# Another order of all engines, one load per block at the head, fewer tiny steps and quarter columns at the end of a hybrid decoder layer

## The chip, the cores and the metric

The kernel runs on one core of a Trainium2 chip. The core has a matrix engine (TensorE, PE in the profile), a vector engine (VectorE, DVE), a scalar engine (ScalarE, ACT), GpSimd (POOL) and SyncE (SP), which here only issues transfers; GpSimd issues some as well. The metric is the device time of one execution in microseconds (us), the median over several runs. Everything is fp32 at the interface.

## What is computed

One decoder layer for 512 tokens of width 1024. One combined projection of x feeds two causal mixers; they are merged by gates, projected, added to x and normalised; a gated MLP with a short convolution follows, with a second residual and norm.

```python
h = x @ w_in                                   # q, 6 key/value sets, gates, GDN q/k/v, beta, decay, gate, merge gates
nsa = nsa_attention(...)                       # 8 heads of 64: compressed, selected and window branches, per-head gates
gdn = gated_deltanet(...)                      # 4 heads of 128, chunks of 64, conv 4, triangular solve, gated RMSNorm
mix = sigmoid(g1) * (nsa @ w_nsa_out) + sigmoid(g2) * (gdn @ w_gdn_out)
x = layer_norm(alpha * x + mix @ w_o, ln1_g, ln1_b)
u = causal_dwconv(x @ w_up, conv_w)            # 2 x 2816 columns, width 3
ffn = (act(u[..., :2816]) * u[..., 2816:]) @ w_down
out = layer_norm(alpha * x + ffn, ln2_g, ln2_b)
```

## The kernel before, in words

**Products.** An fp32 operand is split into a rounded high part and the remainder (`split_block`, L447 to L454; `split_w`, L460 to L471; `split`, L1176 and L1177): ScalarE rounds, VectorE subtracts. Each product is then three matmuls, high × high (L481), low × high (L483) and high × low (L484, all in `product`). A full matmul has a moving operand of 512 columns.

**Head.** `load_all` (L433 to L437) loads the transposed x in eight blocks of 128 rows (`xr`), the first two in halves, and beside them the 288 columns of those weights that need the output token by token (`wB`), one block or two at a time. `token_major` multiplies each block with them for four tiles of 128 tokens into the PSUM tiles `pb` (L536 to L538, 12 matmuls a block). Small tables are loaded among these: `tiny` (convolution taps, decays and the like), `pos`, `ident` (for transposes), `fcw`, `cst`.

**Projections and mixers.** `gemm_t` makes one unit of the combined projection: it loads 512 KB of weights (`raw`), splits them and runs 24 matmuls a tile into a PSUM buffer `gps`, of which there are two. Between these units lie the small steps of DeltaNet (`gdn_k`, `gdn_q`, `gdn_v`, `gdn_mid`, the triangular solve with `xs` and `z` at L769 to L772, `gdn_out` with 128-wide matmuls at L837 to L861, `gdn_gate` with `so`, `y` and `yT`) and of the attention (scores L1039 and L1040, softmax `sc` L1043 to L1056, transposes L1072, products with v L1086 and L1092). Most of their matmuls are 64 to 256 wide.

**Merge.** For each of eight channel pairs, two `gps` units give the gate by a tanh (L1118, on ScalarE, into `mt`), the two mixers' outputs are projected into the PSUM tiles `pm0` and `pm1`, VectorE multiplies them in (L1196, one for each) and adds the two (L1198). The tile `mt` is then free for another unit's tanh, and that tanh frees a `gps` buffer.

**o-products and FFN.** The output projection runs as fast-product halves of seven sub-products into `pu` and `pw` (L1285), added into the residual by VectorE at L1290, with its bn_stats at L1292. The up-projection goes the same way; the down-projection is `three` at L1449 into `px` and `pz`, with weight sums formed by transfers on GpSimd's queue. At the end `take` (L1482) adds a 128 × 512 tile of `px` into the residual, `count` takes its bn_stats (L1491), `norm` aggregates (L1241), gets the reciprocal root (L1243, then a power on GpSimd, L522), scales (L1249, L1250) and stores (L1496).

**What sets the order.** The program is written stage by stage, but the order on each engine is not that of the code: QUEUES holds for each engine a list of instruction numbers, and `queues` chains them, so that the scheduler keeps that order. These chains carry no semaphore: an instruction waits on the chip only for its data and buffers.

## Time and profile before

| | us |
|---|---|
| runs | 822.28, 822.27, 820.61 |
| median | 822.27 |
| span of the profiled execution | 820.8 |
| TensorE busy in it | 802.4 (98%) |
| VectorE busy | 600.2 (73%) |
| ScalarE busy | 409.1 (50%) |
| GpSimd busy | 179.7 (22%) |

The profile gives the span of its execution, from the first instruction to the end of the last store; a time that includes what lies around it is known only for the three runs. A row of a table of stretches gives the stretch, its length, then for each engine the busy time and the number of instructions, then TensorE's granted clock, the share of time that the DMA engines were busy, and the rate in GB/s. A timeline row gives start, duration, engine, line, operation, output <- input and shape; several equal instructions in a row are drawn as one, with "x4" at the end; in brackets stands how long the engine had stood idle, and what released it. The queue of transfers is SPq.

### The profile page before, as it was taken

How to read it: one execution, taken by the hardware profiler on the slowest of the kernel's cores; microseconds unless marked ns; L12 is line 12 of the kernel's file. 1: busy time of each engine (PE TensorE's matmuls, PEld its weight loads, DVE VectorE, ACT ScalarE, POOL GpSimd, SP SyncE). 2: the span in 40 equal slices, each digit the busy share in tenths (PEclk: the TensorE clock that was granted, in tenths of full speed). 3: DMA queues.
4: the chain of work that ended last, by engine and by line, in shares of the span. 5: the costliest groups of instructions: out<-in, count | busy, mean ns of one | idle time of the engine just before them, and what ended most of it. 6: DMA issues, size and time to landing. Idle time of an engine off the chain costs nothing.

```text
span 820.8 us, 11781 instructions
## 1 busy us (share of the span) xinstructions
PE 802.4 (98%) x4138; PEld 670.2 (82%) x4138; DVE 600.2 (73%) x1339; ACT 409.1 (50%) x912; POOL 179.7 (22%) x176
## 2 busy tenths in 40 slices
PE   8999999999999999999999999999999999999996
PEld 8788888787888888888787898888888888878784
DVE  5667689979768965556578956666685667777888
ACT  4453587774577764323254234344354444565641
POOL 0244835042365111241200101111111210200000
PEclk9999999999999999999999999999999999999999
DMA  8327280013624942343357387285336492465674
GB/s 282 106 78 267 80 267 30 26 53 97 161 86 103 194 90 77 108 134 123 103 209 226 129 168 243 93 185 146 98 117 210 111 235 91 143 202 178 210 220 149
DMA packets 43978, 119.57 MB, mean 146 GB/s; under 512 B 3472, under 2 KB 4624, under 8 KB 43664
## 3 DMA queue, kind: packets, MB, share of 16 engines
q1 hardware_dynamic: 32144, 87.37, 33.3%
q0 software_dynamic: 11776, 31.46, 16.6%
q8 instruction: 32, 0.52, 0.3%
q14 instruction: 26, 0.21, 0.1%
HBM read 116.72 MB, written 33.55 MB: 183 GB/s over the span
## 4 chain that ended last, share of the span: by engine, by line
PE 79%; DVE 9%; DMA 7%; ACT 2%; issue 2%; SPq 0%; POOL 0%; DVEq 0%; ACTq 0%; POOLq 0%
PE pu L481 9%; PE pu L483 9%; PE pu L484 9%; PE gps L481 9%; PE gps L483 8%; PE gps L484 8%; DMA raw<-wsum 3%; PE pout L1086 2%; PE aps L1072 2%; DMA raw<-in_down 2%; DVE wl L1385 2%; PE pz L1449 2%; PE pm L483 2%; PE pm L481 2%; PE pm L484 2%
## 5 line engine op out<-in xcount | busy, mean ns | idle before, releaser
L471 DVE TENSOR_TENSOR wl<-raw,wh 128x512 fp32r<-128x512 f32 x146 | 103.9, 717 | 73.2 <-ACT wh L467 40.9
L467 ACT ACTIVATE wh<-raw 128x512 fp32r<-128x512 f32 x126 | 79.0, 629 | 138.6 <-PE pu L483 91.4
L484 PE MATMUL pu<-mh,wl 128*128 128x512 f32 (+1 forms) x384 | 129.9, 372 | 0.2 <-DVE wl L471 0.2
L481 PE MATMUL pu<-mh,wh 128*128 128x512 f32 (+1 forms) x384 | 129.8, 372 | 0.0
L483 PE MATMUL pu<-ml,wh 128*128 128x512 f32 (+1 forms) x384 | 129.6, 372 | 0.0
L481 PE MATMUL gps<-xh,wh 128*128 128x512 f32 x320 | 123.5, 399 | 2.4 <-ACT mt L1118 1.5
L483 PE MATMUL gps<-xl,wh 128*128 128x512 f32 x320 | 123.2, 397 | 0.0
L484 PE MATMUL gps<-xh,wl 128*128 128x512 f32 x320 | 122.8, 397 | 0.0
L484 PEld LDWEIGHTS pu<-mh,wl 128*128 128x128 f32 x384 | 71.3, 188 | 13.4 <-DVE wl L471 0.6
L481 PEld LDWEIGHTS pu<-mh,wh 128*128 128x128 f32 x384 | 71.0, 188 | 12.6
L483 PEld LDWEIGHTS pu<-ml,wh 128*128 128x128 f32 x384 | 71.0, 188 | 12.6
L1407 DVE SCALAR_TENSOR_TENSOR fa<-pu,fcw,fa 128x511 f32<-128x511 f32 (+1 forms) x88 | 64.9, 745 | 18.9 <-ACT fa L1404 18.3
L1413 POOL TENSOR_TENSOR fth<-fth,fa 128x512 f32<-128x512 f32 x22 | 31.3, 1428 | 197.3 <-DVE fth L1412 182.8
L481 PEld LDWEIGHTS gps<-xh,wh 128*128 128x128 f32 x320 | 60.0, 188 | 13.5 <-issue 2.9
L484 PEld LDWEIGHTS gps<-xh,wl 128*128 128x128 f32 x320 | 60.0, 188 | 11.0 <-POOL wl L471 0.2
L483 PEld LDWEIGHTS gps<-xl,wh 128*128 128x128 f32 x320 | 60.1, 188 | 10.6
L1384 ACT ACTIVATE wh<-raw 128x512 fp32r<-128x512 f32 x67 | 40.0, 625 | 37.2 <-DMA raw<-wsum 11.4
L1385 DVE TENSOR_TENSOR wl<-raw,wh 128x512 fp32r<-128x512 f32 x67 | 44.5, 691 | 15.8 <-ACT wh L1384 15.3
L1404 ACT ACTIVATE fa<-pu,fcw 128x512 f32<-128x512 f32 x44 | 29.5, 681 | 30.7 <-PE pu L484 29.2
L471 POOL TENSOR_TENSOR wl<-raw,wh 128x512 fp32r<-128x512 f32 x30 | 40.0, 1337 | 13.5 <-ACT wh L467 7.1
L522 POOL TENSOR_TENSOR rs<-rs,minus_half 128x1 f32<-128x1 f32 x8 | 7.6, 949 | 155.9 <-DVE rs L1243 103.2
L1045 ACT ACTIVATE sc<-sc,mn 128x384 f32<-128x384 f32 (+2 forms) x64 | 35.6, 558 | 5.7 <-DVE mn L1043 5.2
(365 smaller groups left out, 1702.1 us busy)
## 6 DMA issues: line engine op xcount, KB each, us to landing
raw<-in_up SPq DMA_DIRECT2D x44, 512.0 KB, 3.7
raw<-in_wT SPq DMA_DIRECT2D x40, 512.0 KB, 3.5
wsum<-in_down POOLq DMA_DIRECT2D x6, 2816.0 KB, 21.7
raw<-wsum SPq DMA_DIRECT2D x20, 512.0 KB, 4.3
raw<-in_down SPq DMA_DIRECT2D x15, 512.0 KB, 3.9
osum<-in_wo POOLq DMA_DIRECT2D x6, 1024.0 KB, 9.4
wsum<-wsum POOLq DMA_DIRECT2D x2, 2816.0 KB, 14.2
raw<-in_wm SPq DMA_DIRECT2D x8, 512.0 KB, 3.5
```

Of the source, the lines that this page charges most:

```text
L467: A.activation(wh, r, AF.Copy)
L471: eng.tensor_tensor(wl, r, wh.bitcast(F32), op=OP.subtract)
L481: i = PE.matmul(ps, wh[k], mh_(k), start=(k == 0), stop=False)
L483: PE.matmul(ps, wh[k], ml_(k), start=False, stop=False)
L484: PE.matmul(ps, wl[k], mh_(k), start=False, stop=(k == n - 1))
L1045: A.activation(s[:, i, :n], s[:, i, :n], AF.Exp, scale=-1.0, bias=mn[:, 0, i:i + 1], accum_out=mn[:, 1, i:i + 1])
L1072: PE.transpose(pt[:, i, k, :], s[:, i, k * 128:(k + 1) * 128], ident)
L1384: A.activation(hi, raw[:, i], AF.Copy)
L1385: V.tensor_tensor(lo, raw[:, i], hi.bitcast(F32), op=OP.subtract)
L1404: A.activation(acc, ps, AF.Copy, scale=w[:, 2:3])
L1407: V.scalar_tensor_tensor(acc[:, n:], ps[:, :S - n], w[:, i:i + 1], acc[:, n:], op0=OP.mult, op1=OP.add)
L1413: G.tensor_tensor(th, th, g[1], op=OP.mult)
```

## The change

It has four parts.

1. *Head loads.* On the host x and the 288 columns are put side by side as `xw`, 800 columns for each block of 128 rows. One transfer of 400 KB brings a block; only the first block comes in three pieces (256, 288 and 256 columns) and is split in halves. The tables move behind the blocks; `pos` becomes 32 columns of `tiny`; the norm's rows are broadcast on the host.
2. *Fewer tiny steps.* `hbeta` is gone. A polynomial of 16 VectorE steps in `decays` takes 9. `norms` becomes `squares`: q's sum of squares isn't turned into a reciprocal root any more, but goes as a term into the one of the output gate, whose chain of five small VectorE steps is now one. `gk` starts from a reciprocal.
3. *Quarter columns at the end.* For the last token tile, the last two pairs of w_down rows are multiplied for 256 columns at a time into `pz0` and `pz1`, and added and counted quarter by quarter; the part before them is taken in as a half as before.
4. *Order.* All five tables of QUEUES are new, and a string TURNS gives one order over all engines, chained in the same way, without semaphores.

The core of the diff, the tables left out but for two lines:

```diff
-        xr = [es.tile([128, S], F32, name=f"xr{k}") for k in range(KD)]
-        raw = [es.tile([128, 2, 288], F32, name=f"wB{k}") for k in range(KD // 2)]
+        xw = [es.tile([128, S + 288], F32, name=f"xw{k}") for k in range(KD)]
         for k in range(KD):
-            n = 2 if k < 2 else 1
-            for i in range(n):
-                ts = slice(i * S // n, (i + 1) * S // n)
-                nc.sync.dma_start(out=xr[k][:, ts], in_=d["xT"][:, k, ts])
-                if i == 0 and k < 2:
-                    nc.sync.dma_start(out=raw[0][:, k], in_=d["wB"][:, k, :])
-                elif i == 0 and k % 2 == 0:
-                    nc.sync.dma_start(out=raw[k // 2], in_=d["wB"][:, k:k + 2, :])
-        return xr, [r[:, i] for r in raw for i in range(2)]
+            for cs in (slice(0, 256), slice(512, 800), slice(256, 512)) if k == 0 else (slice(0, 800),):
+                nc.sync.dma_start(out=xw[k][:, cs], in_=d["xw"][k, :, cs])
+        return [t[:, :S] for t in xw], [t[:, S:] for t in xw]
...
-        V.tensor_scalar(acc, z2, 2.0 / 17, 2.0 / 15, op0=OP.mult, op1=OP.add)
-        for c in (13, 11, 9, 7, 5, 3, 1):
-            V.tensor_tensor(acc, acc, z2, op=OP.mult)
-            V.tensor_scalar(acc, acc, 2.0 / c, None, op0=OP.add)
-        V.tensor_tensor(acc, acc, z, op=OP.mult)
+        V.tensor_scalar(acc, z2, 2.0 / 17, None, op0=OP.mult)
+        for c in (15, 13, 11, 9, 7, 5, 3, 1):
+            V.scalar_tensor_tensor(acc, acc, 2.0 / c, z2 if c > 1 else z, op0=OP.add, op1=OP.mult)
...
-        cq = so[:, 1]
-        V.tensor_scalar(cq, rn, 128.0 ** -0.5, None, op0=OP.mult)
-        t = so[:, 2]
-        V.tensor_tensor(t, cq, cq, op=OP.mult)
-        V.scalar_tensor_tensor(t, t, 1.0 / 128, so[:, 0], op0=OP.mult, op1=OP.mult)
-        V.tensor_scalar(t, t, RMS_EPS, None, op0=OP.add)
+        t = so[:, 1]
+        V.scalar_tensor_tensor(t, so[:, 0], 1.0 / 128, ss, op0=OP.mult, op1=OP.add)
         rsqrt(t, t, TT)
-        V.tensor_tensor(t, t, cq, op=OP.mult)
...
     for t in range(2):
-        for j, w in held:
-            three(px[t], a, j, t, w, False, j == NP - 1)
+        cut = NP - 2 if t else NP
+        for j, w in held[:cut]:
+            three(px[t], a, j, t, w, False, j == cut - 1)
         take(2 + t, left, px[t], OP.add)
-        count(2 + t, 0)
+        if t:
+            for i in range(2):
+                cs = slice(i * 256, i * 256 + 256)
+                for j, w in held[cut:]:
+                    three(pz[i][:, :256], a, j, t, [x[:, cs] for x in w], j == cut, j == NP - 1)
+                more(2 + t, cs, pz[i][:, :256], OP.add)
+                V.bn_stats(out=stats[2 + t][:, i, :], in_=x1[:, 2 + t, cs])
+        else:
+            count(2 + t, 0)
         norm(2 + t)
...
-132 131 133-137 147 150 138-139 142-143 145 153 148 146 149 151-152 154-155 157 156 158-161 163 162 165 164 166-171""",
+135 134 138-139 143 141 146 142 144 149 145 147-148 153 150-152 154 156 155 157 159 158 160-167""",
...
+    chain([next(names[x]) for x, n in re.findall(r"([A-Z])(\d*)", TURNS) for _ in range(int(n or 1))])
```

What the new tables move shows in the order of the instructions. First SP's queue in the head, from the third x block on, before: `xr` and `wB` are the blocks, `ident`, `tiny` and `pos` the tables, the first `raw` the first projection unit's weights.

```order
L433 DMA xr_128<-in_xT 128x512
L437 DMA wB_135<-in_wB 128x576
L566 DMA ident<-in_consts 128x128
L433 DMA xr_129<-in_xT 128x512
L433 DMA xr_130<-in_xT 128x512
L564 DMA tiny<-in_tiny 128x57
L938 DMA pos<-in_pos 128x32
L437 DMA wB_136<-in_wB 128x576
L433 DMA xr_132<-in_xT 128x512
L433 DMA xr_131<-in_xT 128x512
L437 DMA wB_137<-in_wB 128x576
L433 DMA xr_133<-in_xT 128x512
```

The same queue from its first transfer, now:

```order
L488 DMA xw_126<-in_xw 128x288
L488 DMA xw_126<-in_xw 128x256 x2
L488 DMA xw_127<-in_xw 128x800
L488 DMA xw_128<-in_xw 128x800
L488 DMA xw_129<-in_xw 128x800
L488 DMA xw_130<-in_xw 128x800
L488 DMA xw_131<-in_xw 128x800
L488 DMA xw_132<-in_xw 128x800
L488 DMA xw_133<-in_xw 128x800
L511 DMA raw<-in_wT 128x1024
L615 DMA tiny<-in_tiny 128x89
L511 DMA raw<-in_wT 128x1024
```

The blocks now come first and whole, and the tables stand behind the first projection unit's weights. The second place is TensorE in the merge, around the longest wait. `pm0_4603` and `pm1_4617` are one pair's projections, `gps_4566` is the gate unit that runs beside them and `gps_4659` the next unit. Before:

```order
L483 MATMUL pm0_4603<-yol_4024,wh_4595 128x512
L481 MATMUL gps_4566<-xh_93,wh_4562 128x512
L484 MATMUL pm0_4603<-yoh_4005,wl_4597 128x512
L483 MATMUL gps_4566<-xl_94,wh_4562 128x512
L484 MATMUL pm1_4617<-yoh_4005,wl_4601 128x512
L484 MATMUL gps_4566<-xh_93,wl_4564 128x512
L481 MATMUL gps_4566<-xh_93,wh_4562 128x512
L483 MATMUL gps_4566<-xl_94,wh_4562 128x512
L484 MATMUL gps_4566<-xh_93,wl_4564 128x512
L481 MATMUL gps_4659<-xh_93,wh_4651 128x512
```

The same place now, where the pair is `pm0_4552` and `pm1_4566`, the unit beside them `gps_4515` and the next one `gps_4608`; the last matmul of pm1 is the row just ahead of these.

```order
L535 MATMUL gps_4515<-xh_93,wl_4513 128x512
L532 MATMUL gps_4515<-xh_93,wh_4511 128x512
L535 MATMUL pm0_4552<-yoh_3954,wl_4546 128x512
L534 MATMUL gps_4515<-xl_94,wh_4511 128x512
L535 MATMUL gps_4515<-xh_93,wl_4513 128x512
L532 MATMUL gps_4515<-xh_93,wh_4511 128x512
L534 MATMUL gps_4515<-xl_94,wh_4511 128x512
L535 MATMUL gps_4515<-xh_93,wl_4513 128x512
L532 MATMUL gps_4515<-xh_93,wh_4511 128x512
L534 MATMUL gps_4515<-xl_94,wh_4511 128x512
L535 MATMUL gps_4515<-xh_93,wl_4513 128x512
L532 MATMUL gps_4608<-xh_93,wh_4600 128x512
```

Four matmuls of the unit stood between the last projection matmul and the next unit, and eight stand there now; pm1 comes before pm0. Lines L481, L483 and L484 are L532, L534 and L535 in the changed kernel.

More of the change, by code (lines that the diff above doesn't have):

```diff
@@ L340, in queues, with chain @@
             made[k].append(i)
-    for k, runs in QUEUES.items():
-        last = None
-        for run in runs.split():
-            a, _, b = run.partition("-")
-            for n in range(int(a), int(b or a) + 1):
-                i = made[k][n]
-                if last is not None:
-                    tc.add_manual_dep(i, last.name, mybir.DependencyInfo(
-                        mybir.DependencyClass.NoSync, mybir.DependencyReason.SCHED_ONLY), reason="place in its queue")
-                last = i
+    def chain(items):
+        for a, b in zip(items, items[1:]):
+            tc.add_manual_dep(b, a.name, mybir.DependencyInfo(
+                mybir.DependencyClass.NoSync, mybir.DependencyReason.SCHED_ONLY), reason="place in its queue")
+    rows = {}
+    for k, runs in QUEUES.items():
+        ends = [r.partition("-")[::2] for r in runs.split()]
+        rows[k] = [made[k][n] for a, b in ends for n in range(int(a), int(b or a) + 1)]
+        chain(rows[k])
+    for p in PINS.split():
+        i, j = (int(n) for n in p.split(":"))
+        tc.add_manual_dep(made["Pool"][i], made["DVE"][j].name, mybir.DependencyInfo(
+            mybir.DependencyClass.Sync, mybir.DependencyReason.DATA), reason="begins behind it")
+    names = {"G" if k == "Pool" else k[0]: iter(r) for k, r in rows.items()}
+    chain([next(names[x]) for x, n in re.findall(r"([A-Z])(\d*)", TURNS) for _ in range(int(n or 1))])
 @with_exitstack
@@ L588, in body @@
     eg = nsa.tile([128, 3, TT, GH], F32, name="eg")
-    nbe = nsa.tile([128, TT, GH], F32, name="nbe")
     def decays():
@@ L936, in compressed @@
         nc.sync.dma_start(out=w2, in_=d["w2"])
-        pos = nsa.tile([128, 2, 16], F32, name="pos")
-        nc.sync.dma_start(out=pos, in_=d["pos"])
+        pos = tiny[:, 57:89].rearrange("p (i n) -> p i n", i=2)
         V.memset(kv[:, 4], 0.0)
@@ L1229, in rows_of, with layer_norm @@
     def rows_of(t, o):
[L1230 to L1231 removed]
+        nc.sync.dma_start(out=t, in_=d["lnr"][:, o:o + 2, :])
     rows_of(ln1, 0)
     moments = {}
[L1237 removed]
+    def layer_norm(r, gb, st, after=lambda cs: None, halves=(0, 1)):
         if 0 in halves:
@@ L1250, in layer_norm @@
             V.scalar_tensor_tensor(r[:, cs], r[:, cs], rs, gb[:, 1, cs], op0=OP.mult, op1=OP.add)
-            after(i)
+            after(cs)
     ps3 = ExitStack()
@@ L1486, in more @@
         V.tensor_tensor(r, r, ps, op=op)
-    stats = [ln.tile([128, 2, 6], F32, name=f"st{t}") for t in range(TT)]
+    stats = [ln.tile([128, 4 if t == TT - 1 else 2, 6], F32, name=f"st{t}") for t in range(TT)]
     def count(t, i):
-        V.bn_stats(out=stats[t][:, i, :], in_=x1[:, t, i * 512:(i + 1) * 512])
+        n = stats[t].shape[1]
+        w = 1024 // n
+        for j in range(i * n // 2, (i + 1) * n // 2):
+            V.bn_stats(out=stats[t][:, j, :], in_=x1[:, t, j * w:(j + 1) * w])
     def norm(t, halves=(0, 1)):
```

496 lines of the change are left out of this document (271 added, 225 removed), and 3 rows, old and new, of the table QUEUES.

## The prediction

> **What bounds the kernel now.** I read the page's busy times first, then a table of stretches that cover the span from 4.8 us on, then the list of TensorE's (PE's) waits, and last the timeline around each of those waits. The table gives, for each stretch, its length and then the busy time of each engine.
>
> ```profile
> PE   802.4 (98%) x4138; PEld 670.2 (82%) x4138; DVE 600.2 (73%) x1339; ACT 409.1 (50%) x912; POOL 179.7 (22%) x176
> ...
> 4.80:20.00 15.20, 13.76 (x97) 13.09 (x97) 9.39 (x19) 7.45 (x16) 0.29 (x1) 1.00 0.93 329
> 20.00:456.00 436.00, 429.49 (x2369) 358.71 (x2368) 325.81 (x892) 242.00 (x628) 134.62 (x136) 1.00 0.43 126
> 456.00:812.50 356.50, 355.44 (x1661) 295.00 (x1659) 258.27 (x416) 157.48 (x265) 43.13 (x33) 1.00 0.57 161
> 812.50:820.80 8.30, 0.38 (x2) 0.00 (x0) 4.81 (x9) 0.00 (x0) 0.92 (x1) 0.80 0.50 191
> ```
>
> TensorE is the bound: 802.4 of 820.8 us. A change of order can win only what it leaves idle. That is 15.20 − 13.76 = 1.44 us in the head, 436.00 − 429.49 = 6.51 us from there to the FFN, and 356.50 − 355.44 = 1.06 us in the FFN. The tail of 8.3 us after the last matmul is the final norm and the store. So the largest gain open to any order of the same work is 1.44 + 6.51 + 1.06 = 9.0 us, 1.1% of the time, plus what the tail can give. The clock (the column after the five engines) is 1.00 wherever TensorE works, so there is nothing to win there. The list of waits says where most of the 9 us stand.
>
> ```profile
> PE gps L481 <- ACT mt L1118: 1.5, 1, 1.5
> ...
> PE gps L481 <- issue: 0.9, 1, 0.9
> ...
> PE pb L536 <- ACT xh L447: 0.8, 1, 0.8
> PE dps L736 <- DVE yT L892: 0.7, 1, 0.7
> PE pu L1285 <- DVE x L1290: 0.7, 1, 0.7
> PE pb L536 <- ACT wh L452: 0.7, 1, 0.7
> ```
>
> Each is one wait at one place (in us: in total, times, longest), so each can be priced by itself; two more, of 0.84 and 1.08 us, have their rows below.
>
> **The change part by part.** All terms are against this execution's span of 820.8 us; the median of the runs, 822.27, lies 1.47 above it, and I add that at the end.
>
> *Head loads.* The two head waits sum to 0.8 + 0.7 us. The second is a late x tile.
>
> ```profile
> 5.90 0.43 SPq L564 DMA_DIRECT2D tiny<-in_tiny  x1
> ...
> 13.08 0.43 PE L537 MATMUL pb<-wl,xh 128*128 128x288 f32 x2
> 13.34 0.42 PE L538 MATMUL pb<-wh,xl 128*128 128x288 f32 x2
> 13.42 1.33 ACT L447 ACTIVATE xh<-xr 128x512 fp32r<-128x512 f32 x2 [1.27 <-DMA xr<-in_xT]
> ...
> 14.80 0.53 PE L536 MATMUL pb<-wh,xh 128*128 128x288 f32 x2 [0.77 <-ACT xh L447]
> ```
>
> ScalarE stood 1.27 us for the transfer, and TensorE then stood 0.77 us for ScalarE. Small tables were issued between the x loads, and one issue holds SP's queue for 0.43 us. After the change the eight blocks follow each other without a table between. One block is 128 × 800 × 4 = 409,600 bytes; at the 329 GB/s of the second row of the table above that is 1.25 us. TensorE needs longer for a block: three products for each of four row tiles are 12 matmuls, and two of them take 13.34 − 13.08 = 0.26, so 6 × 0.26 = 1.6 us. The loads therefore stay ahead and both waits should go: bound 0 to −1.44. I take **−1.2**, near the whole, since the first block's pieces can still come late. If the cover is gone (a block at 1.6 us or more) the gain is 0. The moved tables are not needed until the first convolution and transposes.
>
> [...]
>
> *Fewer tiny steps.* DVE has 1311 instructions instead of 1339 and four reciprocal roots fewer lie on POOL. DVE is busy 600 of 821 us; a removed instruction pays only where TensorE waits for that chain. In the decays no matmul of the list waits for the polynomial, so that is 0. The gate chain ends in yT, for which TensorE waits 0.7 us; it loses one step before y, but the new order leaves 16 wide matmuls rather than 21 between the last DeltaNet output and the y transposes, which takes away about as much cover: 0 (bounds −0.7 to +0.7).
>
> *Order, place one: scores beside the triangular solve.* Two waits, 0.8 and 1.1 us, at 155 to 159 us.
>
> ```profile
> 155.02 0.33 PE L1072 MATMUL aps<-ident,sc 128*128 128x128 f32 x1 [0.84 <-DVE sc L1056]
> ...
> 158.13 0.69 DVE L772 TENSOR_TENSOR z<-xs,cst 128x512 f32<-128x512 f32 x1
> ...
> 158.88 0.55 PE L656 MATMUL dps<-ident,z 128*128 128x128 f32 x3 [1.08 <-DVE z L772]
> ```
>
> DVE is the late one here, with the substitution's tiny steps and the scores' steps in turn. Between the scores matmul ahead of this stretch and the first z transpose TensorE has 15 wide and 11 narrow matmuls in the new order, against 13 and 9: 2 × 0.23 + 2 × 0.11 = 0.68 us more cover (the rows of these two durations are quoted at the switches below). Two more small scores steps on DVE ahead of z take some back. Between −1.9 and 0 I take **−0.5**.
>
> *Place two: the merge.* Here is the longest wait. pm is a PSUM tile that DVE must add into mt before ScalarE can overwrite the gate with the next tanh, which frees the PSUM buffer that TensorE wants.
>
> ```profile
> 395.00 1.29 DVE L1196 SCALAR_TENSOR_TENSOR mt<-mt,pm 128x512 f32<-128x512 f32 x2 [3.18 <-PE pm L484]
> 395.03 0.39 PE L484 MATMUL pm<-yoh,wl 128*128 128x512 f32 x1
> ...
> 396.32 0.69 DVE L1198 TENSOR_TENSOR mt<-mt 128x512 f32<-128x512 f32 x1
> 397.05 0.60 ACT L1118 ACTIVATE mt<-gps 128x512 f32<-128x512 f32 x1 [7.86 <-DVE mt L1198]
> ...
> 397.79 0.47 PE L481 MATMUL gps<-xh,wh 128*128 128x512 f32 x1 [1.47 <-ACT mt L1118]
> ```
>
> From the last pm matmul at 395.03 to the next unit's first at 397.79 pass 2.76 us, and TensorE had that matmul and four more, 5 × 0.23 = 1.15: lost 1.61. In the new order eight stand behind the last pm matmul, cover 9 × 0.23 = 2.07. The other pm tile is now finished three matmuls earlier (0.68 us), so DVE has its addition (1.29 / 2 = 0.65) done when the last one arrives, and the chain from the last pm is 0.42 + 0.65 + 0.73 (396.32 to 397.05) + 0.74 (397.05 to 397.79) = 2.54. Wait left 2.54 − 2.07 = 0.5, gain **−1.1** (0 to −1.6).
>
> *Place three: the o-products.* The wait of 0.7 us for L1290.
>
> ```profile
> 439.09 0.69 DVE L1292 BATCH_NORM_STATS2 sa<-x 128x6 f32<-128x512 f32 x1
> 439.70 1.27 DVE L1290 SCALAR_TENSOR_TENSOR x<-pu,x 128x512 f32<-128x512 f32 x2
> 440.51 0.47 PE L1285 MATMUL pu<-woh,ah 128*128 128x512 f32 x1 [0.72 <-DVE x L1290]
> ```
>
> The two pu buffers are freed by L1290. The new order has 13 matmuls instead of 7 between the last pu0 of one product and the first of the next, 6 × 0.23 = 1.4 us more cover against 0.7 of wait, and takes the statistics from between: **−0.7** (0 to −0.7). The wait of 0.9 us for "issue" at 38 us keeps its cover, and I leave it.
>
> *Switches between narrow and wide matmuls.* The new order cuts the small matmuls into more runs: from a narrow one to a 512-wide one TensorE goes 197 times instead of 135, 62 more. Does a switch cost?
>
> ```profile
> 48.30 0.27 PE L656 MATMUL dps<-ident,kq 128*128 128x128 f32 x1
> 48.33 0.47 PE L481 MATMUL gps<-xh,wh 128*128 128x512 f32 x1
> 48.64 0.39 PE L483 MATMUL gps<-xl,wh 128*128 128x512 f32 x1
> 48.87 0.40 PE L484 MATMUL gps<-xh,wl 128*128 128x512 f32 x1
> ...
> 171.04 0.60 PE L656 MATMUL dps<-ident,kq 128*128 128x128 f32 x4
> ...
> 171.71 0.40 PE L481 MATMUL gps<-xh,wh 128*128 128x512 f32 x1
> ```
>
> Wide ones follow at 48.87 − 48.64 = 0.23. One narrow and one wide take 48.64 − 48.30 = 0.34, so the narrow one adds 0.11. Four and a wide one take 171.71 − 171.04 = 0.67, so again 0.11 each ((0.67 − 0.23) / 4). By these starts a switch is free; but a wide one behind a narrow one is drawn 0.47 long instead of 0.39, so the upper bound, rounded up, is 0.09. I take a hundredth, near the starts: 62 × 0.01 = **+0.6** (0 to +5.6).
>
> *Column halves at the end.* The statistics chain behind the last matmul is short now.
>
> ```profile
> 812.49 0.39 PE L1449 MATMUL px<-w,pl 128*128 128x512 f32 x1
> 812.91 0.69 DVE L1482 SCALAR_TENSOR_TENSOR x<-x,px 128x512 f32<-128x512 f32 x1
> 813.64 0.69 DVE L1491 BATCH_NORM_STATS2 st<-x 128x6 f32<-128x512 f32 x1
> 814.37 0.21 DVE L1241 BATCH_NORM_AGGREGATE mv<-st 128x2 f32<-128x12 f32 x1
> ...
> 461.00 0.28 PE L481 MATMUL pu<-mh,wh 128*128 128x256 f32 x1
> 461.12 0.28 PE L483 MATMUL pu<-ml,wh 128*128 128x256 f32 x1
> ...
> L1418 DVE TENSOR_TENSOR pl<-fth,ph 128x256 fp32r<-128x256 f32 x11 | 4.6, 418 | 2.3 <-ACT ph L1417 2.3
> ```
>
> Now 814.37 − 812.49 = 1.88 us. In the new order eight 256-wide matmuls follow the last 512-wide one L, about 8 × (461.12 − 461.00) = 1.0. DVE adds the whole half from L + 0.42 to L + 1.11, then the two quarters at 0.42 each to L + 1.95, then two statistics at 0.42, with 0.04 between, to L + 2.85. The last matmul starts at L + 1.1 and half a wide matmul later than before, so the aggregate comes 2.85 − 1.1 + 0.11 = 1.86 us after the old instant: even. Twelve halves at 0.12 for six at 0.23 add 0.1. So **+0.1** (−0.3 to +0.4): two halves done in turn cost on DVE what they save.
>
> [...]
>
> *Sum:* −1.2 − 0.5 − 1.1 − 0.7 + 0.6 + 0.1 = −2.8 us. Span 818.0, time 822.27 − 2.8 = **819.5 us**, 0.34% less.
>
> **The rivals.** *Every wait goes.* With DVE shorter by 28 steps and an order that fits the measured durations, the 1.44 + 6.51 us before the FFN could all go at no price for switching: 822.27 − 7.95 + 0.1 = 814.4. For it: each wait is single and has work nearby that could cover it. Against it: place two keeps 0.5 by its own rows, and the 38 us wait keeps its cover.
>
> *The waits only move.* TensorE is busy 98%, and each place has DVE at work nearly all the time; with another order the same number of waits stands elsewhere. Only the head's loads help: −1.2 + 0.6 + 0.1 = −0.5, time 821.8. For it: at 154 to 160 us DVE, not the order on TensorE, is late. Against: places two and three have counted cover.
>
> *Switching costs.* If the longer drawing of the first wide matmul is real time, 62 × 0.09 = 5.6, and the sum is −3.4 + 5.6 = +2.2: 824.5 us, slower. It decides from 3.4 / 62 = 0.055 us a switch (no gain left) and is measurably slower from (3.4 + 1.64) / 62 = 0.08. For it: 0.47 against 0.39. Against it: the starts, which show none of it.
>
> **How the numbers follow.** 0.2%, 1.64 us, is about what a measurement of this kernel can tell from no change: below 820.6 is faster, above 823.9 slower. My forecast 819.5 has a chance of 0.42, every wait gone 0.18, waits only moved 0.24, switching 0.16. So faster 0.42 + 0.18 = 0.60, same 0.24, slower 0.16. The range goes from the first rival's 814.4 to the third's 824.5, which takes in the bounds of the unknown switching cost up to its upper row. The likeliest case's own range, with the bounds of its terms, is 817.5 to 821.
>
> **What would show it.** In the changed kernel's profile: no TensorE wait above 0.3 us for xh or wh in the first 20 us, and the last head matmul about 1.2 us earlier; the wait for the tanh of mt at 0.5 or less; none for L1290's new line; the stretch from the head to the FFN with about 4 us idle instead of 6.5; and the last matmul to the aggregate still near 1.9. The prediction is wrong if the starts of a narrow and a following wide matmul lie more than 0.34 apart, if new waits of a microsecond stand in the DeltaNet steps, or if TensorE's busy time has grown by more than 1.

## The result, and the profile after

| | us |
|---|---|
| runs after | 816.1 to 817.55 (four) |
| median after | 816.37 |
| median before, beside it | 822.27 |
| ratio | 0.9944, interval 0.9932 to 0.9957 |
| span of the profiled execution | 814.3 (before 820.8) |

The changed kernel is faster by 0.56% (0.43 to 0.68%), 4.6 us by the ratio. The two medians alone would give 5.9 us, but in four further sets of runs the kernel before had medians of 820.01 to 820.65, so its 822.27 stands high, and the ratio is the figure used here. The forecast said 0.34%, 2.8 us: right in its direction and inside its range, too small in its size. Of the likeliest case's own range, 817.5 to 821, the median 816.37 lies below the lower end; 0.9944 of 822.27, 817.7, lies just inside. The sum was also right for partly wrong reasons, as the experiments show.

First the busy times of the changed kernel's page, and its table of stretches with cuts at the same places of the program.

```profile
PE 800.0 (98%) x4144; PEld 670.2 (82%) x4144; DVE 595.8 (73%) x1314; ACT 409.1 (50%) x911; POOL 177.3 (22%) x172
```

```profile
4.80:20.00 15.20, 14.60 (x103) 13.81 (x103) 9.96 (x22) 7.92 (x18) 0.00 (x0) 1.00 0.86 331
20.00:456.00 436.00, 431.92 (x2381) 359.56 (x2380) 325.49 (x868) 242.61 (x629) 132.44 (x135) 1.00 0.43 126
456.00:806.00 350.00, 350.00 (x1650) 293.49 (x1648) 254.63 (x414) 157.15 (x264) 43.77 (x32) 1.00 0.58 163
806.00:814.30 8.30, 0.09 (x1) 0.00 (x0) 4.48 (x10) 0.00 (x0) 0.92 (x1) 0.75 0.60 232
```

TensorE's idle time in the head is 0.60 us instead of 1.44, from there to the FFN 4.08 instead of 6.51, and in the FFN nothing instead of 1.06. That is 4.3 us in all, but the span is 6.5 us shorter. So idle time as the page draws it does not hold the whole gain, and a second measure is needed.

The list of TensorE's waits in the changed kernel:

```profile
PE gps L605 <- DVE vm L602: 1.4, 1, 1.4
PE dps L703 <- DVE vraw L699: 1.0, 1, 1.0
PE aps L1112 <- DVE tmp L815: 0.9, 1, 0.9
PE gps L532 <- issue: 0.9, 1, 0.9
PE gps L532 <- ACT mt L1158: 0.5, 1, 0.5
PE pb L587 <- ACT xh L498: 0.5, 1, 0.5
PE gps L532 <- DVE kl L950: 0.2, 1, 0.2
```

The first stands ahead of the head and was 1.4 before too. The waits for `z`, `yT`, `x` and `wh` are gone, the one for the tanh of `mt` is a third as long, and `vraw` (109 us) and `tmp` (155.7 us) are new, about a microsecond each; `kl` is new too, with 0.2.

**The second measure.** Matmuls overlap (in the rows below one of 512 columns is drawn 0.39 us long, and the median distance to the next start is 0.227), so the drawn length of one is not what it costs. Between the starts of two matmuls lies a usual distance, which depends on the shape of the first: the medians of the trace of before, used for both kernels, are 0.227 us for 512 columns, 0.120 for 256, 0.132 for 288, 0.11 for 128. Whatever a start comes later than that is lost. Summed over the timeline's 4,138 rows of before this gives 29.8 us lost up to the last matmul, and 22.9 over the 4,144 of after: 6.9 us less, close to what the span shows (6.5 shorter, with a tail 0.2 longer and twelve 256-wide matmuls in place of six 512-wide ones). The FFN's longest stall in before shows the difference from drawn idle time:

```profile
724.50 1.35 POOL L1413 TENSOR_TENSOR fth<-fth,fa 128x512 f32<-128x512 f32 x1 [10.75 <-DVE fth L1412]
...
725.89 0.43 DVE L1425 TENSOR_TENSOR sr<-fth 128x256 f32<-128x256 f32 x1 [1.19 <-POOL fth L1413]
726.08 0.39 PE L1449 MATMUL pu<-wh,ph 128*128 128x512 f32 x1
726.23 0.68 DVE L1385 TENSOR_TENSOR wl<-raw,wh 128x512 fp32r<-128x512 f32 x1
...
726.97 0.50 PE L1449 MATMUL pu<-wl,ph 128*128 128x512 f32 x1 [0.51 <-DVE wl L1385]
...
727.31 0.39 PE L1449 MATMUL pu<-wh,pl 128*128 128x512 f32 x1
```

Drawn: 0.51 us idle. By starts: 726.97 − 726.08 − 0.23 = 0.66, and the next matmul follows after 0.34 instead of 0.23, so 0.77 us in all. VectorE stood for GpSimd's product, then did the sum `sr` ahead of the weights' low part `wl` for which TensorE waited.

Here is the loss by stages of TensorE's work, in us. The column "others of old order" has three variants of before that follow below: norm rows spread on the host, a shorter gate chain, and one exchange in the FFN. "Others of new order" are a second profile of the changed kernel and two variants of it: norm rows broadcast on the chip, and full halves at the end.

| stage (time, about) | before | others of old order | after | others of new order |
|---|---|---|---|---|
| up to 82 | 8.2 | 7.2, 7.6, 7.5 | 7.4 | 7.1, 7.2, 7.2 |
| to 218 | 10.2 | 10.2, 11.2, 10.3 | 9.9 | 9.9, 9.9, 9.9 |
| to 392 | 4.1 | 5.3, 4.3, 5.5 | 4.4 | 4.5, 4.9, 4.4 |
| merge, to 409 | 1.7 | 1.8, 1.8, 1.7 | 0.8 | 0.8, 0.8, 0.8 |
| o-products, first norm and the first products of the FFN, to 502 | 2.7 | 1.9, 1.7, 2.4 | 0.6 | 0.6, 0.6, 0.6 |
| rest of the FFN | 2.9 | 1.6, 1.9, 1.7 | −0.1 | −0.2, 0.3, −0.1 |

Two things are read off. The last three stages bring most of the gain, and the largest part lies in the FFN, for which the prediction had no term. And stages differ between executions of one order by up to a microsecond and more: the profile of before has the largest loss of its four in the head, the o-products and the FFN. A cost that a stage has everywhere, such as a switch between narrow and wide matmuls (0.025 us on average in the run on switches below), is in these losses too.

Now the places of the prediction. The head's first x blocks, after:

```profile
4.70 0.72 ACT L498 ACTIVATE xh<-xw 128x256 fp32r<-128x256 f32 x2 [2.70 <-DMA xw<-in_xw]
...
5.48 0.40 PE L587 MATMUL pb<-wh,xh 128*128 128x288 f32 x1 [0.48 <-ACT xh L498]
...
7.90 0.63 ACT L498 ACTIVATE xh<-xw 128x512 fp32r<-128x512 f32 x1 [0.88 <-DMA xw<-in_xw]
...
8.51 0.29 PE L589 MATMUL pb<-wh,xl 128*128 128x288 f32 x1
...
8.92 0.67 PE L587 MATMUL pb<-wh,xh 128*128 128x288 f32 x3
```

TensorE waits at 5.48, and at 8.92 it starts 0.41 after the matmul ahead of it instead of 0.13. ScalarE still stands for a block, 0.88 us. The merge:

```profile
393.04 1.37 DVE L1236 SCALAR_TENSOR_TENSOR mt<-mt,pm 128x512 f32<-128x512 f32 x2 [4.27 <-PE pm L535]
...
393.30 0.39 PE L535 MATMUL pm<-yoh,wl 128*128 128x512 f32 x1
...
394.44 0.82 DVE L1238 TENSOR_TENSOR mt<-mt 128x512 f32<-128x512 f32 x1
...
395.30 0.60 ACT L1158 ACTIVATE mt<-gps 128x512 f32<-128x512 f32 x1 [7.25 <-DVE mt L1238]
...
396.04 0.47 PE L532 MATMUL gps<-xh,wh 128*128 128x512 f32 x1 [0.54 <-ACT mt L1158]
```

From the last pm matmul to the next unit's first pass 2.74 us with nine matmuls of cover, 9 × 0.227 = 2.04: 0.70 lost instead of 1.61. The new wait at 109 us:

```profile
107.88 0.42 DVE L1083 CUSTOM_DVE_ANT_0 sc<-aps,cst 128x256 f32<-128x256 f32 x1
...
108.22 0.69 DVE L699 SCALAR_TENSOR_TENSOR vraw<-th,acc 128x512 f32<-128x512 f32 x1
...
109.05 0.41 PE L703 MATMUL dps<-ident,vraw 128*128 128x128 f32 x2 [1.01 <-DVE vraw L699]
```

VectorE does a score's step first, then the convolution's product that TensorE wants. And the end:

```profile
804.67 6.34 SPq L1538 DMA_DIRECT2D out_dram<-x  x8
...
805.80 0.28 PE L1488 MATMUL pz<-w,pl 128*128 128x256 f32 x1
806.01 0.75 DVE L1525 TENSOR_TENSOR x<-x,pz 128x256 f32<-128x256 f32 x2
806.68 0.74 DVE L1592 BATCH_NORM_STATS2 st<-x 128x6 f32<-128x256 f32 x2
807.46 0.26 DVE L1280 BATCH_NORM_AGGREGATE mv<-st 128x2 f32<-128x24 f32 x1
```

Last matmul to aggregate: 1.66 us (before 1.88). Aggregate to the end of the span: 814.3 − 807.46 = 6.84 (before 820.8 − 814.37 = 6.43).

### The profile page after: what moved, and what is told of

It is laid out like the page before. It is cut to its first block, busy times and chain, and to the rows that moved or that the text cites. A ratio compares the mean times of both kernels' runs of the same rounds, so it can differ in the third digit from the quotient of the medians.

```text
span 814.3 us, 11754 instructions
## 1 busy us (share of the span) xinstructions
PE 800.0 (98%) x4144; PEld 670.2 (82%) x4144; DVE 595.8 (73%) x1314; ACT 409.1 (50%) x911; POOL 177.3 (22%) x172
## 4 chain that ended last, share of the span: by engine, by line
PE 93%; DVE 3%; ACT 1%; DMA 1%; issue 1%; SPq 0%; DVEq 0%; ACTq 0%
PE pu L532 10%; PE pu L535 10%; PE pu L534 10%; PE gps L532 8%; PE gps L535 8%; PE gps L534 8%; PE px L1488 7%; PE pz L1488 4%; PE pw L1324 3%; PE pout L1126 2%; PE aps L1112 2%; PE pu L1324 2%; PE pu L1488 2%; PE pm L532 2%; PE pm L534 2%; PE pm L535 2%
## 5 line engine op out<-in xcount | busy, mean ns | idle before, releaser
L532 PE MATMUL pu<-mh,wh 128*128 128x512 f32 (+1 forms) x384 | 131.5, 373 | 0.0
L534 PE MATMUL pu<-ml,wh 128*128 128x512 f32 (+1 forms) x384 | 131.2, 373 | 0.0
L535 PE MATMUL pu<-mh,wl 128*128 128x512 f32 (+1 forms) x384 | 129.5, 373 | 0.0
L532 PE MATMUL gps<-xh,wh 128*128 128x512 f32 x320 | 124.8, 401 | 1.8 <-issue 0.9
L535 PE MATMUL gps<-xh,wl 128*128 128x512 f32 x320 | 126.4, 402 | 0.0
L534 PE MATMUL gps<-xl,wh 128*128 128x512 f32 x320 | 124.2, 399 | 0.0
L535 PEld LDWEIGHTS pu<-mh,wl 128*128 128x128 f32 x384 | 71.3, 188 | 13.1
L534 PEld LDWEIGHTS pu<-ml,wh 128*128 128x128 f32 x384 | 71.5, 188 | 12.6
L532 PEld LDWEIGHTS pu<-mh,wh 128*128 128x128 f32 x384 | 71.0, 188 | 12.7 <-ACT mh L1303 0.2
L532 PEld LDWEIGHTS gps<-xh,wh 128*128 128x128 f32 x320 | 60.1, 189 | 13.5 <-issue 2.6
L535 PEld LDWEIGHTS gps<-xh,wl 128*128 128x128 f32 x320 | 60.1, 189 | 10.5 <-DVE wl L522 0.2
L534 PEld LDWEIGHTS gps<-xl,wh 128*128 128x128 f32 x320 | 60.0, 188 | 10.5
L573 POOL TENSOR_TENSOR rs<-rs,minus_half 128x1 f32<-128x1 f32 x8 | 9.4, 1175 | 154.0 <-DVE rs L1282 154.0
L1443 ACT ACTIVATE fa<-pu,fcw 128x512 f32<-128x512 f32 x44 | 29.8, 680 | 20.4 <-PE pu L535 18.8
```

The lines of the kernel that those rows point to most:

```text
L532: i = PE.matmul(ps, wh[k], mh_(k), start=(k == 0), stop=False)
L534: PE.matmul(ps, wh[k], ml_(k), start=False, stop=False)
L535: PE.matmul(ps, wl[k], mh_(k), start=False, stop=(k == n - 1))
```

## The experiments

Each is a variant of before or of after. Where an order is exchanged, the rows of QUEUES that belong to a stage take the relative order of the other kernel, on all five engines, at the places that this stage's instructions had; the order of the rest stays. Five variants of after leave the string TURNS out: those with the FFN's or the merge's order, the head or the end of before, and the one with two steps moved.

**The FFN's order alone, put into before.** Of the tables the end of GpSimd's, the shortest, shows the kind of edit.

```diff
     "Pool": """...
-132 131 133-137 147 150 138-139 142-143 145 153 148 146 149 151-152 154-155 157 156 158-161 163 162 165 164 166-171""",
+132 131 133-137 139 138 142-143 147 145 150 146 148 153 149 151-152 157 154-156 158 160 159 161 163 162 164-171""",
...
```

> The kernel before with only the order of the FFN's instructions (from the second group of up-projection columns to the end, on all five engines) taken from the changed kernel; head, mixers, merge and o-products keep their old order, and the end keeps its 512-wide halves. Theory (the FFN order gave some 3 us, which the drawn idle time of 1.06 us hid, because a matmul behind a stall starts its successor later too): 822.3 - 3.0 = 819.3 us, and by starts no stall above 0.1 us left between 500 and 800 us. Rival one (what the trace of before draws as idle is all that can be won): 822.3 - 1.1 = 821.2. Rival two (the stalls in the FFN come from the transfers' phase or from the time at which the stage begins, not from the order): no change, 822.3, with stalls at other places.

Measured: 818.92 against 820.55, ratio 0.9978 (0.9969 to 0.9988): 1.8 us, less than the 3.0 expected. The loss in the rest of the FFN is 1.0 instead of 1.6 to 2.9, and the stall at 500 us is gone, but stalls of 0.29 and 0.24 stay at 725 us. So this order is worth time by itself, though no term of the prediction had it.

**The FFN's order of before, put into after.** The same edit in the other direction.

> The changed kernel with the FFN's instructions in the old relative order (the quarter columns at the end kept where they stand); the chain over all engines is left out. Theory (FFN order worth 3 us): 816.4 + 3.0 = 819.4 us, with the stalls of before at the same places (behind the split of w_down weights on VectorE that stands behind a step that waits for GpSimd). Rival one (idle as drawn): 817.5. Rival two (phase, not order): 816.4.

Measured: 819.33, ratio 0.9981 (0.9972 to 0.9989), against the changed kernel's 0.9944 (a second time 0.9956): 2 to 3 us come back. Stalls stand again at 497.3, 723.8, 730.1, 761.0 and 761.9 us, at the places where before has them some 3 us later, with 0.25 to 0.42 each, and one of 0.29 at 801.5 that before doesn't have; the stage loses 2.65. Its timeline at the place shown above:

```profile
723.04 0.69 DVE L1376 TENSOR_TENSOR wl<-raw,wh 128x512 fp32r<-128x512 f32 x1
723.13 0.39 PE L1440 MATMUL pu<-wh,ph 128*128 128x512 f32 x1
...
723.78 0.50 PE L1440 MATMUL pu<-wl,ph 128*128 128x512 f32 x1 [0.26 <-DVE wl L1376]
...
724.11 0.39 PE L1440 MATMUL pu<-wh,pl 128*128 128x512 f32 x1
```

0.65 and 0.33 between the starts, so 0.42 + 0.10 lost, and again `wl` is the late operand. Both directions agree: the FFN's order is the largest single part of the gain.

**One exchange in before's FFN.** Is it a few neighbours? `wl` and the sum `sr` change places on VectorE at 726 us.

```diff
     "DVE": """...
-1101 1147 1150 1153 1134 1149 1112 1114 1135 1155-1156 1102 1126 1158-1159 1136 1125 1138 1161 1139 1115 1137
+1101 1147 1150 1153 1134 1149 1112 1114 1135 1155-1156 1102 1126 1158-1159 1136 1125 1161 1138-1139 1115 1137
```

> The kernel before with two neighbours on VectorE exchanged, at 726 us: the split of w_down weights (L1385), for which TensorE waits there, now stands ahead of the FFN's sum (L1425), which waits 1.19 us for GpSimd with the split queued behind it. Nothing else moves. Theory (a step that waits for GpSimd at the head of VectorE's queue makes the next split late, and the new FFN order gains by having no such pair): TensorE's stall at 727 us (0.67 by starts, or 0.34, in the executions so far) goes, the others in the FFN (733, 741 to 765 us) stay; the time falls by 0.3 to 0.7 us, too little to be told from none. Rival (the weights themselves come late): the stall stays, and VectorE stands idle for the rounding on ScalarE instead.

Measured: 820.96 against 820.65, ratio 1.0007 (0.9998 to 1.0015).

```profile
726.44 0.39 PE L1449 MATMUL pu<-wh,ph 128*128 128x512 f32 x1
726.71 0.41 DVE L1425 TENSOR_TENSOR sr<-fth 128x256 f32<-128x256 f32 x1
...
726.84 0.50 PE L1449 MATMUL pu<-wl,ph 128*128 128x512 f32 x1
...
727.18 0.40 PE L1449 MATMUL pu<-wh,pl 128*128 128x512 f32 x1
```

The stall falls from 0.66 to 0.17, but 0.16 appears at 729 and the one at 733 grows from 0.32 to 0.45; the stage loses 1.65, inside the spread of the old order. One stall taken out by hand gains nothing that can be measured; the gain is that of the whole order.

**The order of the merge, the o-products and the first norm of before, put into after.** The edit is as with the FFN.

> The changed kernel with the instructions of the last merge pairs, the o-products, the first norm and the x1 transposes in the old relative order; the rest as changed, the chain over all engines left out. Theory (by starts the new order won 1.0 us at the merge and 2.0 us from there to the first up-projection): 816.4 + 3.0 = 819.4 us, the wait for the tanh of mt back at about 1.5 us and the one for the addition of pu at about 0.7. Rival (only the two waits as the prediction priced them, 1.1 + 0.7): 818.2. Rival two (the waits only move and come back elsewhere): 816.4 to 817.

Measured: 817.35, ratio 0.9960 (0.9947 to 0.9973), not told from after's by the intervals and well short of the 819.4 expected. The trace is clearer.

```profile
395.92 0.60 ACT L1111 ACTIVATE mt<-gps 128x512 f32<-128x512 f32 x1 [8.38 <-DVE mt L1191]
...
396.66 0.47 PE L485 MATMUL gps<-xh,wh 128*128 128x512 f32 x1 [1.46 <-ACT mt L1111]
```

The merge's wait is back at 1.46, and the stage loses 1.75 as before. In all thirteen profiles of the layer this stage loses 1.7 to 1.8 with the old order and 0.8 with the new, so the term is confirmed in the trace; in time, 1 us is too little to be told from none by these intervals. But in the o-products, with the old order, next to nothing is lost: 0.4 up to 502 us. The stalls of before there, at 440, 445 and 453 us, are not the order alone.

**The norm's rows.** If it is not the order, it may be the loads around them: in before 1 MB of the norm's rows (`ln`) is read with a broadcast and lands a median of 8.1 us after its issue, after the change 6.0. First before with the rows spread on the host, then after with the broadcast of before.

```diff
-        "lnr": np.stack([g("ln1_g")[0], ...]),
+        "lnr": np.broadcast_to(np.stack([g("ln1_g")[0], ...]), (128, 4, 1024)),
...
-        nc.sync.dma_start(out=t, in_=bass.AP(tensor=d["lnr"].tensor, ..., ap=[[0, 128], [D, 2], [1, D]]))
+        nc.sync.dma_start(out=t, in_=d["lnr"][:, o:o + 2, :])
```

> The kernel before with one edit: the rows of the two norms are spread over the 128 partitions on the host, so that their load (1 MB, twice) reads 128 different rows instead of the same 8 KB 128 times. All orders stay. Theory (the wait of the o-products for the addition into the residual is a late transfer: it stood behind the split of w_o, that behind its load, and that load shared the DMA engines with the norm rows, which took 9.6 us to land and 6.0 in the changed kernel): the stall at 440 us (0.88 by starts) and those at 445 and 453 (0.34 and 0.30) shrink or go, 1 to 1.5 us faster, 821.0 where before is 822.3. Rival (the new order of TensorE's o-products cured it, as the prediction had it): no change, the stall stays at 0.9.

> The changed kernel with the norm rows spread on the chip again (1 MB from the same 8 KB, twice), all orders as changed. It is the counterpart of the kernel before with the rows spread on the host, which was not faster. By starts TensorE loses 1.7 to 2.7 us between the merge and the first up-projection in four executions of the old order and 0.6 in the new, also with the old relative order of the o-products. Theory one (where the loads stand among the other transfers and splits decides): the loss there stays at 0.6 within 0.2, and the time at 0.995 of before. Theory two (the slower landing of the norm rows holds the w_o loads back, and the old order only hid it among its other late loads): the loss there comes back to 1.5 or more, 0.996 of before or worse.

Measured: before with spread rows 820.83 against 820.62, ratio 0.9999 (0.9991 to 1.0008), with 1.9 us lost in the stage. After with the broadcast 816.68 against 820.01, ratio 0.9960 (0.9947 to 0.9974), with 0.64 lost. Neither moves, so nothing shows the rows to be the cause; spreading them changed their landing little as well (a median of 7.5 us in the first, 7.3 with the broadcast in the second). What is, the list of ScalarE's waits between 425 and 447 us tells in part. It rounds the weights `woh` there, from loads (`raw`). The two rows for loads in before:

```profile
ACT woh L1171 <- DMA raw<-in_wo: 3.0, 1, 3.0
ACT woh L1171 <- DMA raw<-osum: 2.9, 2, 2.6
```

The only such row in after with the old order of this stage:

```profile
ACT woh L1164 <- DMA raw<-osum: 0.4, 1, 0.4
```

And that of after with the broadcast, which has the new order:

```profile
ACT woh L1211 <- DMA raw<-in_wo: 2.6, 1, 2.6
```

In all five profiles with before's own queues ScalarE stands 5.3 to 5.9 us in all for these loads, VectorE is late behind it, and TensorE loses. With the old order but the loads in time (0.4) TensorE loses 0.4 there, and with the new order and a late load (2.6) it loses 0.6, no more than the changed kernel itself, whose ScalarE stands 1.9 there for a load of `osum`. So it looks as if a stall needs both, the order without cover and late loads; but the late load under the new order is half as late as those of before, so the order's part is argued and not shown. Why the loads of `osum` land a median of 5.4 to 5.9 us after their issue in every profile of before's queues and 4.5 or 4.6 in every one of after's is not settled. It isn't the time of issue alone: counted from the merge's tanh wait, the hybrid issues its first load of `in_wo` about 0.5 us earlier than before, but the second one at the same time, and that lands after 4.6 us instead of 7.5.

**The head's loads of before, put into after.**

```diff
-            for cs in (slice(0, 256), slice(512, 800), slice(256, 512)) if k == 0 else (slice(0, 800),):
-                nc.sync.dma_start(out=xw[k][:, cs], in_=d["xw"][k, :, cs])
+            n = 2 if k < 2 else 1
+            for i in range(n):
+                ts = slice(i * S // n, (i + 1) * S // n)
+                nc.sync.dma_start(out=xr[k][:, ts], in_=d["xw"][k, :, ts])
+                if i == 0 and k < 2:
+                    nc.sync.dma_start(out=raw[0][:, k], in_=d["xw"][k, :, S:])
...
```

> The changed kernel with the head loads as before: x blocks and the 288 columns in separate transfers, the first two blocks in halves, ident and tiny between the blocks, and the old order of the head's splits and matmuls; the rest as changed, the chain over all engines left out. Prediction's step (the new loads win 1.2 us): 816.4 + 1.2 = 817.6 us, and TensorE loses 1.2 us more in the first 20 us. Rival (the head of the one execution profiled before was a late one: by starts old loads lost 5.2 us in one execution and 4.1 in another, new ones 4.0 to 4.8 in four): no change within 0.4 us, 816.4.

Measured: 815.97, ratio 0.9945 (0.9932 to 0.9957), the changed kernel's own ratio. The loads are worth nothing that can be measured in time. In the first 20 us the six profiles with before's loads show waits for xh and wh of 0.8 and 0.7 (before), 0.5 and 0.3, 0.3 and 0.4, 0 and 0.3, and none at all in two; the seven with the new loads show one wait for xh of 0.2 to 0.9. By starts the first lose 4.2 to 5.2 us there, with before the highest, and the second 4.0 to 4.8. The wait of 1.5 us that the prediction removed was one execution's.

**A shorter gate chain in before.** The part "fewer tiny steps" where it could reach TensorE, the chain ahead of yT.

```diff
-        cq = so[:, 1]
-        V.tensor_scalar(cq, rn, 128.0 ** -0.5, None, op0=OP.mult)
-        t = so[:, 2]
-        V.tensor_tensor(t, cq, cq, op=OP.mult)
-        V.scalar_tensor_tensor(t, t, 1.0 / 128, so[:, 0], op0=OP.mult, op1=OP.mult)
-        V.tensor_scalar(t, t, RMS_EPS, None, op0=OP.add)
+        t = so[:, 1]
+        V.scalar_tensor_tensor(t, so[:, 0], 1.0 / 128, ss, op0=OP.mult, op1=OP.add)
...
```

> The kernel before with only the output gate's chain shortened: q's sum of squares goes into the one reciprocal root of the gate (one VectorE step instead of five around it, and one root less on GpSimd per head); the order of all engines stays otherwise. Prediction's step (worth 0, the cover decides): 822.3, the waits for y and yT at 189 to 194 us still there. Rival (the chain decides: 16 steps of 0.15 to 0.17 us fewer, two to four of them on the path to yT): the stalls there, 0.43 + 0.90 by starts, shrink by 0.5 to 1.3 us, 821.0 to 821.8.

Measured: 821.08, ratio 1.0007 (0.9997 to 1.0017). The wait for yT stays at 0.90 by starts; the one for y (0.43) goes, and a new one of 1.11 stands at 102.4 us, behind another VectorE step (`cs`). Zero, as the prediction had it.

**The full halves at the end, put into after.**

```diff
-        cut = NP - 2 if t else NP
-        for j, w in held[:cut]:
-            three(px[t], a, j, t, w, False, j == cut - 1)
+        for j, w in held:
+            three(px[t], a, j, t, w, False, j == NP - 1)
         take(2 + t, left, px[t], OP.add)
-        if t:
...
-        else:
-            count(2 + t, 0)
+        count(2 + t, 0)
```

> The changed kernel with 512-wide halves at the end as before: the last two pairs of w_down rows go into px as 6 matmuls of 512 columns behind the others, one addition and one bn_stats for the half; the chain over all engines left out. Theory of the prediction (two quarters done in turn cost on VectorE what they save, and 0.1 us on TensorE): between -0.3 and +0.3 us of 816.4, not to be told from it, and in the trace 1.9 us from the last matmul to the aggregate. Rival (the quarters shorten the end): 0.5 us or more slower, 816.9. Rival two (the quarters cost, since the stores of the last two token tiles now come closer together): 0.3 to 0.5 us faster, 816.0.

Measured: 816.77, ratio 0.9953 (0.9941 to 0.9965), not told from after's 0.9944. From the last matmul to the aggregate pass 1.88 us, as expected, and from there to the end of the span 6.82. So the quarters save 0.2 us behind the last matmul, against 0.1 on TensorE, and the longer end behind the aggregate isn't theirs. TURNS, which is left out here too, does not carry the gain.

**What a switch costs.** A kernel of nothing but matmuls, with as many narrow and wide ones in each stretch, cut into few or many runs.

```python
for i in range(4):       # 4 runs of 16 narrow ones
    wide(64)
    narrow(16)
for i in range(64):      # 64 runs of one
    wide(4)
    narrow(1)
```

> Computes nothing of the layer: it returns x and only times TensorE. Five stretches of the same work, 256 matmuls of 512 columns, four of them with 64 transposes of 128 columns: narrow ones in runs of 16 behind 64 wide ones (4 runs), one behind every 4 wide ones (64 runs), 4 behind every 16 (16 runs), one in the middle of every 4 (64 runs), and none. Theory of the prediction (by the starts a switch is nearly free, 0.01 us): every mixed stretch takes 256 x 0.227 + 64 x 0.111 = 65.2 us within 0.6. Rival (a switch costs the 0.09 us by which the next wide one is drawn longer): the stretches with 64 runs take 5.4 us more than that with 4.

Measured by starts, in one execution: 256 wide and 64 narrow take 65.04 us in 4 runs, 65.74 in 16, 66.54 in 64, and 66.65 in the other stretch with 64. So (66.54 − 65.04) / 60 = 0.025 us for each further run on average; the first 12 cost 0.70 and the next 48 only 0.80, so the price isn't the same for each. A period of it in the timeline:

```profile
111.19 0.27 PE L54 MATMUL ps<-ident,x 128*128 128x128 f32 x1
111.21 1.17 PE L47 MATMUL pw<-r 128*128 128x512 f32 x4
112.22 0.27 PE L54 MATMUL ps<-ident,x 128*128 128x128 f32 x1
```

1.03 us for four wide and one narrow, where 4 × 0.227 + 0.11 = 1.02. At this average the 62 more switches cost about 1.5 us, an estimate: more than the 0.6 taken, and less than half of the 0.055 for each that would have left no gain.

**The changed kernel a second time, and with two steps of VectorE moved.** Both new waits stand behind VectorE. The step that makes `vraw` is put ahead of its neighbours, and so are two steps of the scores at 155 us.

```diff
     "DVE": """...
-... 321 190 188 191 174 152 ...
+... 321 174 190 188 191 152 ...
...
-... 286 253 311 287 308 288
-309 289 312 ...
+... 286 253 308-309 311
+287-289 312 ...
```

> The changed kernel as it is, once more, beside the runs of before on this chip and beside the next kernel. All theories expect the ratio of the first measurement, 0.9944, within its interval of 0.9932 to 0.9957; for the trace, the theory that the stalls of the order come back in every execution and those of the transfers do not expects the stalls at 37, 109, 156 and 396 us at the same sizes (1.1, 1.2, 1.1, 0.7) and the head's to differ.

> The changed kernel with two moves on VectorE, against the two largest stalls that its order still has: at 108 us the product vraw, for which TensorE waits, ahead of three steps of the attention's scores; at 154 us the reciprocal and the scaling of a scores tile ahead of the next tile's scores step. The chain over all engines is left out. Theory (these stalls are VectorE's order): the stall at 109 us falls from 1.18 to 0.4 or less and that at 156 from 1.12 to 0.4 or less, 1.4 us in all, 0.9927 of before where the changed kernel has 0.9944. Rival (the waits only move, since VectorE has no slack there): stalls of the same sum appear behind them, and the time is the changed kernel's.

Measured: a second time 817.02, ratio 0.9956 (0.9943 to 0.997); with the moves 817.14, ratio 0.9956 (0.9943 to 0.9968). The stalls at 109, 155 and 396 us are the same in the second profile of the changed kernel to 0.02 us, so they belong to the order; of the long ones only those in the head differ. With the moves the wait for vraw is gone and the one at 155 us is split into these:

```profile
PE aps L1065 <- ACT sc L1047: 0.4, 2, 0.3
PE aps L1065 <- DVE sc L1049: 0.3, 1, 0.3
```

By starts the stage loses 10.2 instead of 9.9: at 109 to 110 us 0.24 and 0.28 stand where 1.17 stood, but at 155 to 160 us 0.50, 0.27, 0.43 and 0.42 where 1.12 and 0.15 stood, and the rest goes in smaller pieces. VectorE has next to no slack here (in the changed kernel it is busy 5.9 of the 6 us from 104 and 5.8 of those from 154), and a step put forward makes another late. None of the variants is measurably faster than the changed kernel.

## Why the prediction was right and wrong

**The merge, −1.1: right.** Measured −0.95 by starts, with 0.54 drawn as left against 0.5 forecast. Counting the cover (nine matmuls instead of five) against the chain of four steps was enough; the chain took 2.74 us instead of 2.54, mostly because the sum L1238 lasted 0.82 rather than 0.69.

**Scores and solve, −0.5: right in size, with the rival's mechanism in it.** The stage lost 10.2 to 10.3 in three profiles of the old order (11.2 with the shorter gate chain) and 9.9 in the new: −0.4. But the waits for z and yT went and those for vraw and tmp came, as the rival "the waits only move" had it for VectorE's places. The sign "new waits of a microsecond in the DeltaNet steps", which was to prove the prediction wrong, did appear; it did not decide the sum. Of the other signs, the stretch up to the FFN has its 4 us of drawn idle time (4.08) and the line of L1290 has no wait, but xh still has 0.48 in the head, where at most 0.3 was to be left.

**Fewer tiny steps, 0: right in size**, by the variant of before with the shorter chain; the shorter polynomial and `gk` had no run of their own. The waits for `y` and `yT`, which this term left as they were, did go in the changed kernel: the shorter chain alone took only the first, so the new order has a part in the second. VectorE has 1314 instructions on the page, 25 fewer and not 28.

**Head loads, −1.2: wrong.** The step that failed is "the loads therefore stay ahead and both waits should go". ScalarE still stands 0.88 us for a block at 7.90, and the loads of before in the changed kernel cost nothing. Above all the price was read from one execution: it shows 1.5 us of these waits, the five others with before's loads that are listed above 0.8, 0.7, 0.3 and twice none. Blocks of 400 KB here were no faster than pieces of 128 to 288 KB (0.9944 and 0.9945), and no slower either.

**O-products, −0.7: the sign right, the reason incomplete.** The wait at 440 us was taken for a matter of the order. By the runs it doesn't come from the order alone, late loads go with it, and it comes and goes between executions of the old order (0.88, 0.59, 0.21, none, none by starts). The term was also too small: the stalls at 445 and 453 us, which go with the same lateness on ScalarE and VectorE, were not counted. Of the stage's 2.2 (median of the old order) the FFN's order holds 0.5 (1.06 against 0.59 with it put back), about 1.1 remain. They came with the whole change: with only this stage's old order put back, none of it returned (0.4).

**The FFN, no term: the largest error.** The step that failed is the reading of the table of stretches: "1.06 us in the FFN" was named as the limit there and then left out of the sum, because the list of waits showed nothing long. The loss by starts is 1.6 to 2.9 in the rest of the FFN and 0.5 at its beginning, in half a dozen stalls of 0.2 to 0.7 us. Each is drawn shorter than it is (the longest 0.51 for 0.66), and where a stall has 0.2 us or more the next matmul comes late too, after 0.31 to 0.34 us instead of 0.227. The new order removes nearly all of them, worth 1.8 to 3.0 us in time.

**Switches, +0.6: mis-sized.** Starts gave a free switch within their rounding; the run gives 0.025 each on average, 1.5 us by estimate. The rival "switching costs" is out, by the faster kernel and by this price: the longer drawing of the first wide matmul (0.47 for 0.39) is for the most part not time.

**Quarter columns, +0.1: not to be told from 0.** From the last matmul to the aggregate "still near 1.9" was forecast, and 1.66 was measured: the sum took each quarter's step at its drawn 0.42, but two of them start 0.34 apart. The end behind the aggregate came 0.4 later. Together the tail is 814.3 − 805.80 = 8.50 instead of 8.31. The last store takes 2.46 us from issue to landing instead of 2.01; with full halves the end behind the aggregate is as long (6.82). Why is not settled.

**The sum.** From the medians of the table, old order against new, the change takes 0.35 us off each of the first three stages, 0.95 off the merge, 1.55 off the o-products with the first products of the FFN and 1.9 off the rest of the FFN: 5.45. With 0.1 for the quarter matmuls and 0.2 for the tail that leaves 5.1, inside the measured interval (3.5 to 5.6) and above its middle. The price of the switches is already inside these losses and must not be added again. Of the three times 0.35 only the second, to 218 us, is clear of the spread between executions. Single losses below 0.25 us sum to 16.4 us before and 14.5 after, in spite of the switches, and no run here takes them apart. So the forecast's sum is no further off because two errors ran against each other, 1.2 us in the head that weren't there and about 2.4 in the FFN that had no term; that part is luck.

**The rival "every wait goes".** The measured ratio 0.9944 lies between the forecast's 0.9966 (819.5 of 822.27) and the 0.9904 of this rival (814.4), nearer to the forecast; by the median, 816.4, it is nearer to the rival. Its way isn't borne out either: it had no gain in the FFN, and 4.1 us of idle time stayed ahead of the FFN.

## What to carry to other kernels

Where one engine is busy 98% by the page, sum its losses from start to start, stage by stage, and against the usual distance of each shape: half a dozen stalls of 0.2 to 0.7 us, which the list of waits put last or left out, were the largest item here. A wait behind a transfer in one profile is a sample (that for xh was 0.8 us in before and none with the spread rows), so look at a second execution before it gets a price; the long waits of the mixers and the merge, at 109, 155 and 396 us, came again to 0.02 us in the second profile of the changed kernel. And where the engine that is waited for had next to no slack (busy 5.9 and 5.8 of 6 us), moving one of its steps forward only moved the wait, in both places where it was tried.

## What the hardware showed beyond that

In the profiles of before and after, 15 matmuls of 512 columns start 0.2 us or more late by starts, ten and five, and each is followed after 0.30 to 0.34 us instead of 0.227, so each such stall cost about 0.1 more than its own gap; with the FFN's order of before in the changed kernel the one at 723.78 is followed after 0.33. In the kernel of nothing but matmuls each further run of 128-wide ones among the 512-wide cost 0.025 us on average, (66.54 − 65.04) / 60. And up to 82 us the kernels with before's head lost 7.1 to 8.2 us and those with the new one 7.1 to 7.9, two profiles of the changed kernel itself 7.4 and 7.1. Of the waits that differ, in the first 20 us, the one for xh at 14.80 in before stands behind a load for which ScalarE stood 1.27 us, and that at 5.48 in after behind one of 2.70.
